# A hybrid decoder layer on one core: the first product's loads issued ahead, row loads on another queue, x scaled a chunk earlier, the keys' scale moved to the logits

## The chip, the cores and the metric

The kernel runs on one core of a Trainium2 chip. The metric is device time of one execution in microseconds; lower is better. Before the change it took 1237.17 us (median of three runs, 1237.11 to 1239.0).

## The reference

One layer of a decoder with three parallel branches: x and mem are (256, 2048), everything is float32. Only what matters here:

```python
h = rms_norm(x, norm_w);  proj = h @ w_in              # w_in: 2048 x 18464, split by columns
o_sb  = stick_breaking_attention(q, k, v) * silu(z)    # 8 heads of 128
o_ssd = gated_group_rms_norm(ssd_chunked_scan(...), z) # 32 heads, conv of 4 taps ahead
mem_n = rms_norm(mem, mem_norm_w)
kv = mem_n @ w_kv;  k, v = split(kv, 2)                # 2048 x 2048, 4 heads of 256
probs = softmax(einsum(q, k) * 256 ** -0.5);  o_mem = (probs @ v) * silu(z)
merged = g_sb * (o_sb @ w_sb) + g_ssd * (o_ssd @ w_ssd) + g_mem * (o_mem @ w_mem)
return rms_norm(x + merged @ w_out, final_norm_w)
```

## The kernel before

Every weight is read once, in chunks of 512 KB. To keep float32 precision a chunk is split: ScalarE writes its rounded high part `wh`, VectorE subtracts that from the chunk and writes the low part `wl` (`split`, L144 and L148, for scaled operands L150), and TensorE adds three products, high x high, high x low and low x high, in PSUM. A `gemm` (L238) gives 512 output columns with the tokens on the partitions: per k tile of 128 two token halves, three matmuls each (L257 to L259). A `gemm_cols` (L209) gives 256 columns transposed (L223, L227).

The order of work is written out by hand; every engine executes its instructions in that order. `gemm` and `gemm_cols` go through their chunks; each chunk loads (`load_chunk`, on SP's DMA queue), splits, multiplies and calls `pump`, which runs what has been deferred to that chunk with `defer(fn, chunks)` and one step of a queue of smaller work. A load goes into one of four buffers (`raw`, RAWB = 4) and so waits until the chunk four before has been split; `wh` and `wl` have three buffers each. Loads of all queues take turns on eight completion semaphores, so that no more than eight are in flight.

The start of the program, on which the change bears:

- The first `gemm` (memory values, columns 1024 to 1535 of `w_mem_kv`) runs over ten chunks, four of one k tile and six of two. `along0` splits the mem columns of the same k tiles (`memT`) and issues the load of the next ones. At k tile 6 it also issues two small loads, `wcols` and `drow`. From k tile 10 on each chunk issues a load of mem rows (`row_squares`), on ScalarE's DMA queue; ScalarE squares and sums them three chunks later.
- The second `gemm` (eight chunks) loads the last mem rows and four pieces of x rows in the same way (`along1`). Row tiles have two buffers of each of two kinds, so every load reuses the buffer of the row tile four loads before.
- Four `gemm_cols` give the keys `kT`. Meanwhile `scale_x` and `scale_pair` (L390) take x, transposed, through its norm, two k tiles at a time: VectorE multiplies by `rbc_x` (L392), ScalarE writes the high part of `hT`, VectorE the low part. The keys are scaled by mem's norm, `rbc_m`, as they leave PSUM (L275).
- `mem_head` (L512) reads the logits from PSUM: maximum, exponential with sum, division.
- At the end `last_cols` adds the residual and sums the squares, the last addition of `msy` on GpSimd (L857); `write_out` takes the power of it there (L863), scales in five pieces on VectorE and ScalarE and stores each.

## Time and profile before

| | |
|---|---|
| median of three runs | 1237.17 us |
| the profiled execution, its own time | 1237.6 us |
| its span, first to last instruction | 1235.9 us |
| TensorE busy | 1221.2 us (99%), 6224 matmuls |
| weight loads into TensorE busy | 1037.7 us (84%) |
| VectorE, ScalarE, GpSimd busy | 769.2 (62%), 616.6 (50%), 93.8 (8%) us |
| moved by DMA | 240.58 MB, mean 195 GB/s |
| chain that ended last, by engine | TensorE 93%, DMA 4%, VectorE 1%, ScalarE 1% |

The busy times overlap. The chain follows the execution back from its last instruction, at each step to what released it. Matmuls are pipelined: the duration of one (0.39 us for 512 columns) is longer than the step from one start to the next, and the step is what counts. "Granted clock" is the share of TensorE's full clock; 1.00 is the upper of its two levels, 2.4 GHz, and 0.5 the lower, 1.2 GHz.

### The profile page before, as it was taken

How to read it: one execution, taken by the hardware profiler on the slowest of the kernel's cores; microseconds unless marked ns; L12 is line 12 of the kernel's file. 1: busy time of each engine (PE TensorE's matmuls, PEld its weight loads, DVE VectorE, ACT ScalarE, POOL GpSimd, SP SyncE). 2: the span in 40 equal slices, each digit the busy share in tenths (PEclk: the TensorE clock that was granted, in tenths of full speed). 3: DMA queues.
4: the chain of work that ended last, by engine and by line, in shares of the span. 5: the costliest groups of instructions: out<-in, count | busy, mean ns of one | idle time of the engine just before them, and what ended most of it. 6: DMA issues, size and time to landing. Idle time of an engine off the chain costs nothing.

```text
span 1235.9 us, 16263 instructions
## 1 busy us (share of the span) xinstructions
PE 1221.2 (99%) x6224; PEld 1037.7 (84%) x6224; DVE 769.2 (62%) x995; ACT 616.6 (50%) x797; POOL 93.8 (8%) x108
## 2 busy tenths in 40 slices
PE   8999999999999999999999999999999999999996
PEld 7888888888888888888888888888888888888886
DVE  5587565455644555888878767576756554555554
ACT  6755544554444554544665655455555444444443
POOL 0000000000000000010100202023101110110101
PEclk9999999999999999999999999999999999999998
DMA  9956566654566656556566756666565666567673
GB/s 312 356 179 191 167 190 188 187 171 146 165 198 190 185 173 187 170 173 185 172 187 194 221 177 210 199 199 197 179 183 181 199 196 202 187 198 242 206 235 109
DMA packets 167869, 240.58 MB, mean 195 GB/s; under 512 B 10320, under 2 KB 93680, under 8 KB 167664
## 3 DMA queue, kind: packets, MB, share of 16 engines
q1 hardware_dynamic: 159232, 224.01, 58.7%
q10 hardware_dynamic: 8560, 15.54, 3.8%
q8 instruction: 48, 0.79, 0.3%
q14 instruction: 29, 0.24, 0.1%
HBM read 237.40 MB, written 2.13 MB: 194 GB/s over the span
## 4 chain that ended last, share of the span: by engine, by line
PE 93%; DMA 4%; DVE 1%; ACT 1%; issue 0%; SPq 0%; ACTq 0%; POOLq 0%; POOL 0%; DVEq 0%
PE acc L223 23%; PE acc L258 17%; PE acc L259 17%; PE acc L257 17%; PE acc L227 12%; PE y L741 1%; DMA raw<-in_w_mem_kv_dram 1%; DMA mraw<-in_mem_cols_dram 1%; DMA raw<-in_w_out_dram 1%; DVE wl L148 1%; DMA xraw<-in_x_cols_dram 1%; ACT wh L144 0%; PE acc L910 0%; PE off L743 0%; PE acc L912 0%; PE acc L911 0%
## 5 line engine op out<-in xcount | busy, mean ns | idle before, releaser
L148 DVE TENSOR_TENSOR wl<-raw,wh 128x1024 fp32r<-128x1024 f32 (+1 forms) x410 | 505.5, 1236 | 334.9 <-ACT wh L144 332.4
L144 ACT ACTIVATE wh<-raw 128x1024 fp32r<-128x1024 f32 (+1 forms) x410 | 431.3, 1054 | 420.4 <-PE acc L259 258.3
L223 PE MATMUL acc<-hT,wh 128*128 128x512 f32 x1152 | 363.2, 397 | 0.0
L227 PEld LDWEIGHTS acc<-hT,wl 128*128 128x128 f32 x1152 | 216.4, 188 | 51.2
L257 PE MATMUL acc<-wh,hT 128*128 128x512 f32 x576 | 227.8, 396 | 0.0
L227 PE MATMUL acc<-hT,wl 128*128 128x256 f32 x1152 | 226.6, 278 | 0.0
L259 PE MATMUL acc<-wh,hT 128*128 128x512 f32 x576 | 224.5, 390 | 0.0
L258 PE MATMUL acc<-wl,hT 128*128 128x512 f32 x576 | 224.4, 390 | 0.0
L223 PEld LDWEIGHTS acc<-hT,wh 128*128 128x128 f32 x1152 | 175.5, 189 | 0.1
L259 PEld LDWEIGHTS acc<-wh,hT 128*128 128x128 f32 x576 | 108.1, 188 | 23.0
L258 PEld LDWEIGHTS acc<-wl,hT 128*128 128x128 f32 x576 | 108.3, 188 | 21.8
L257 PEld LDWEIGHTS acc<-wh,hT 128*128 128x128 f32 x576 | 108.2, 188 | 21.6
L257 PE MATMUL acc<-wh,oD 128*128 128x512 f32 x128 | 49.8, 389 | 0.0
L258 PE MATMUL acc<-wl,oD 128*128 128x512 f32 x128 | 49.8, 389 | 0.0
L259 PE MATMUL acc<-wh,oD 128*128 128x512 f32 x128 | 49.8, 389 | 0.0
L667 DVE SCALAR_TENSOR_TENSOR cT<-cu,wcols,cT 128x255 f32<-128x255 f32 (+2 forms) x96 | 46.4, 483 | 3.4
L813 POOL TENSOR_TENSOR merged<-merged,sig 128x512 f32<-128x512 f32 x16 | 27.6, 1743 | 260.3 <-DVE sig L812 233.5
L603 POOL TENSOR_TENSOR lm<-lm,sp 128x384 f32<-128x384 f32 x8 | 11.5, 1432 | 394.5 <-DVE sp L602 392.4
L223 PE MATMUL acc<-memT,wh 128*128 128x512 f32 x128 | 40.7, 399 | 0.1
L257 PE MATMUL acc<-wh,mT 128*128 128x512 f32 x96 | 37.4, 390 | 0.0
L259 PE MATMUL acc<-wh,mT 128*128 128x512 f32 x96 | 37.4, 389 | 0.0
L258 PE MATMUL acc<-wl,mT 128*128 128x512 f32 x96 | 37.4, 389 | 0.0
(248 smaller groups left out, 1305.9 us busy)
## 6 DMA issues: line engine op xcount, KB each, us to landing
raw<-in_w_in_dram SPq DMA_DIRECT2D x288, 512.0 KB, 3.7
raw<-in_w_branch_ssd_dram SPq DMA_DIRECT2D x32, 512.0 KB, 3.9
raw<-in_w_out_dram SPq DMA_DIRECT2D x32, 512.0 KB, 4.8
raw<-in_w_mem_kv_dram SPq DMA_DIRECT2D x30, 512.0 KB, 5.7
raw<-in_w_branch_mem_dram SPq DMA_DIRECT2D x16, 512.0 KB, 4.7
raw<-in_w_branch_sb_dram SPq DMA_DIRECT2D x16, 512.0 KB, 4.0
dec<-acT ACTq DMA_DIRECT2D x16, 256.0 KB, 5.6
sig<-in_b_gate_dram ACTq DMA_DIRECT2D x12, 256.0 KB, 4.0
```

The lines of the kernel that those rows point to most:

```text
L144: nc.scalar.activation(hi, src, AF.Copy, **({} if scale is None else {"scale": scale}))
L148: nc.vector.tensor_tensor(lo, src, h32, ALU.subtract)
L223: nc.tensor.matmul(acc[:, b], wh[:, kt - k0, b * P:(b + 1) * P], lhs.both(kt), start=first, stop=False, skip_group_check=True)
L227: nc.tensor.matmul(acc[:, b, 1], wl[:, kt - k0, b * P:(b + 1) * P], lhs.at(kt)[0], start=False, stop=last, skip_group_check=True)
L257: nc.tensor.matmul(a, lh[:, tt], wh[:, j], start=first, stop=False)
L258: nc.tensor.matmul(a, lh[:, tt], wl[:, j], start=False, stop=False)
L259: nc.tensor.matmul(a, ll[:, tt], wh[:, j], start=False, stop=last)
L603: nc.gpsimd.tensor_tensor(lm, lm, sp, ALU.subtract)
L667: nc.vector.scalar_tensor_tensor(a[:, s:T], u[:, 0:T - s], convw[:, 3 - s, i:i + 1], a[:, s:T], ALU.mult, ALU.add)
L741: nc.tensor.matmul(y[:, q, xc], dec[e // 2][:, e % 2, q], xs[:, q, xc], start=True, stop=True)
L813: nc.gpsimd.tensor_tensor(merged[t][:, cs], merged[t][:, cs], sig[:, t], ALU.add)
```

## The change

It has five parts. The ten weight loads of the first `gemm` and the mem column loads are issued ahead of everything else, four of the weight loads (k tiles 4 to 11) into two tiles of their own (`own`) instead of the four shared buffers; the keys' tiles `kT` are allocated after that product. Row loads go to SP's queue, and their squares are deferred by four chunks. `scale_pair` only scales; the split of the pair follows a chunk later (`split_pair`). The keys are no longer scaled on leaving PSUM; `mem_head` multiplies the logits instead and exponentiates from that copy. In the tail the addition of `msy` moves to VectorE, the division by 2048 into the square, and the five output pieces are cut in another order.

```diff
@@ -200,8 +200,9 @@
     def silu(a, chunks=LATE):
         defer(lambda: nc.scalar.activation(a, a, AF.Silu), chunks)
 
-    def load_chunk(w, c0, width, k0, kc):
-        raw = stage.tile([P, kc, width], F32, tag="raw", name=nm("raw"), bufs=RAWB)
+    def load_chunk(w, c0, width, k0, kc, raw=None):
+        if raw is None:
+            raw = stage.tile([P, kc, width], F32, tag="raw", name=nm("raw"), bufs=RAWB)
         nc.sync.dma_start(
             raw, w[k0 * P:(k0 + kc) * P, c0:c0 + width].rearrange("(k p) n -> p k n", p=P))
         return raw
@@ -235,13 +236,13 @@
         nc.scalar.activation(dst, acc[:, :, 1], AF.Copy)
         nc.vector.tensor_tensor(dst, acc[:, :, 0], dst, ALU.add)
 
-    def gemm(lhs, nk, w, c0, evac, along=None, sizes=None):
+    def gemm(lhs, nk, w, c0, evac, along=None, sizes=None, raws=None):
 
         acc2 = psA.tile([P, 2, GW], F32, tag="acc", name=nm("acc"), bufs=2)
         acc = [acc2[:, 0], acc2[:, 1]]
         k0 = 0
         for kc in sizes or [KC] * (nk // KC):
-            raw = load_chunk(w, c0, GW, k0, kc)
+            raw = raws[k0] if raws else load_chunk(w, c0, GW, k0, kc)
             wh = stage.tile([P, kc, GW], F32R, tag="wh", name=nm("wh"))
             wl = stage.tile([P, kc, GW], F32R, tag="wl", name=nm("wl"))
             split((wh, wl, raw, None))
@@ -267,13 +268,10 @@
             fold(dst[:, b0:b0 + 2], acc)
         return evac
 
-    def to_split_cols(dst, b0, scale=None):
+    def to_split_cols(dst, b0):
         def evac(acc):
             u = tmp.tile([P, 2, T], F32, tag="cu", name=nm("u"), bufs=2)
             fold(u, acc)
-            if scale is not None:
-                nc.vector.tensor_tensor(u, u, scale.unsqueeze(1).to_broadcast([P, 2, T]),
-                                        ALU.mult)
             defer(lambda: split((*dst.at(b0, 2), u, None)), 1)
         return evac
 
@@ -307,10 +305,10 @@
         if q % 2:
             r = [ta([P, GW], "rows") for _ in range(2)]
             for t in range(2):
-                nc.scalar.dma_start(r[t], src[t * P:(t + 1) * P, cs])
+                nc.sync.dma_start(r[t], src[t * P:(t + 1) * P, cs])
             return r
         r = t4([P, 2, GW], "rows")
-        nc.scalar.dma_start(r, src[:, cs].rearrange("(t p) n -> p t n", p=P))
+        nc.sync.dma_start(r, src[:, cs].rearrange("(t p) n -> p t n", p=P))
         return [r[:, t] for t in range(2)]
 
     def squares(r, ss, q):
@@ -342,21 +340,16 @@
     ss_m = const.tile([P, 2, 4], F32, name="ss_m")
     ss_x = const.tile([P, 2, 4], F32, name="ss_x")
 
-    kT = Cols(8, "kT")
     vh = slot([P, 2, 1024], F32R, "vh")
     vl = slot([P, 2, 1024], F32R, "vl")
 
     def along0(k0):
         if k0 == 0:
             split((*memT.at(0), mem0, memw[:, 0:1]))
-            mload(1, 2)
         elif k0 < 4:
             split((*memT.at(k0), mraw[0][:, k0], memw[:, k0:k0 + 1]))
-            mload(k0 + 1, k0 + (3 if k0 == 3 else 2))
         else:
             split_cols(mraw, memT, memw, k0)
-            if k0 < 14:
-                mload(k0 + 2, k0 + 4)
         if k0 == 6:
             nc.sync.dma_start(wcols, w_cols)
             nc.sync.dma_start(drow, d_skip.partition_broadcast(P))
@@ -365,7 +358,7 @@
 
     def row_squares(src, ss, q):
         r = load_rows(src, q)
-        defer(lambda: squares(r, ss, q), 3)
+        defer(lambda: squares(r, ss, q), 4)
 
     def along1(k0):
         if k0 == 0:
@@ -391,6 +384,9 @@
         part = xraw[k // 8][:, k % 8:k % 8 + 2]
         nc.vector.tensor_tensor(part, part, rbc_x.unsqueeze(1).to_broadcast([P, 2, T]),
                                 ALU.mult)
+        defer(lambda: split_pair(k), 1)
+
+    def split_pair(k):
         split_cols(xraw, hT, normw, k)
         x_ready.append(k)
 
@@ -408,11 +404,27 @@
         defer(lambda: lanes[0].append(scale_steps(rs_mem, rbc_m, ss_m)), 1)
         defer(lambda: to_split_rows(vh, vl, 0, rs_mem)(acc), 4)
 
+
+    raws = {}
+    for k in range(4):
+        raws[k] = load_chunk(w_mem_kv, 1024, GW, k, 1)
+        mload(k + 1, k + (3 if k == 3 else 2))
+    for k in range(4, NKT, 4):
+        if k < 12:
+            own = slot([P, 4, GW], F32, "own")
+            raws[k], raws[k + 2] = own[:, 0:2], own[:, 2:4]
+        else:
+            raws[k] = raws[k + 2] = None
+        for j in (k, k + 2):
+            raws[j] = load_chunk(w_mem_kv, 1024, GW, j, 2, raws[j])
+            if j < 14:
+                mload(j + 2, j + 4)
     gemm(memT, NKT, w_mem_kv, 1024, later, along=along0,
-         sizes=[1] * 4 + [2] * 6)
+         sizes=[1] * 4 + [2] * 6, raws=raws)
+    kT = Cols(8, "kT")
     gemm(memT, NKT, w_mem_kv, 1024 + GW, to_split_rows(vh, vl, GW, rs_mem), along=along1)
     for g in range(4):
-        gemm_cols(memT, NKT, w_mem_kv, 2 * g * P, to_split_cols(kT, 2 * g, rbc_m))
+        gemm_cols(memT, NKT, w_mem_kv, 2 * g * P, to_split_cols(kT, 2 * g))
     finish()
 
 
@@ -519,14 +531,15 @@
                 nc.tensor.matmul(lg[:, t], qh, kl, start=False, stop=False)
                 nc.tensor.matmul(lg[:, t], ql, kh, start=False, stop=(d == 1))
         yield
+        pr = ta([P, 2, T], "mpr")
+        nc.vector.tensor_tensor(pr, lg, rbc_m.unsqueeze(1).to_broadcast([P, 2, T]), ALU.mult)
         mx = small([P, 2], "mx")
-        nc.vector.tensor_reduce(mx, lg, AX.X, ALU.max)
+        nc.vector.tensor_reduce(mx, pr, AX.X, ALU.max)
         nmx = small([P, 2], "nmx")
         nc.vector.tensor_scalar(nmx, mx, -1.0 / 16.0, None, ALU.mult)
-        pr = ta([P, 2, T], "mpr")
         sums = small([P, 2], "sums")
         for t in range(2):
-            nc.scalar.activation(pr[:, t], lg[:, t], AF.Exp, bias=nmx[:, t:t + 1],
+            nc.scalar.activation(pr[:, t], pr[:, t], AF.Exp, bias=nmx[:, t:t + 1],
                                  scale=1.0 / 16.0, accum_out=sums[:, t:t + 1])
         rec = small([P, 2], "rec")
         nc.vector.reciprocal(rec, sums)
@@ -853,18 +866,17 @@
                                     ALU.add)
             junk = tq([P, T], "junk")
             q = ssy[:, t, 3 + c // T:4 + c // T]
-            nc.scalar.activation(junk, yc, AF.Square, accum_out=q)
-            nc.gpsimd.tensor_scalar(msy[:, t:t + 1], q, 1.0 / D, msy[:, t:t + 1], ALU.mult,
-                                    ALU.add)
+            nc.scalar.activation(junk, yc, AF.Square, scale=D ** -0.5, accum_out=q)
+            nc.vector.tensor_tensor(msy[:, t:t + 1], q, msy[:, t:t + 1], ALU.add)
             nc.vector.tensor_tensor(yc, yc, fw[:, 3 * GW + c:3 * GW + c + T], ALU.mult)
 
     def write_out(t):
         rs = small([P, 1], "frs")
         nc.gpsimd.tensor_tensor(rs, msy[:, t:t + 1], mhalf[:, 0:1], ALU.pow)
-        for c0, c1, eng, dma in ((0, 512, nc.vector, nc.sync), (512, 896, nc.scalar, nc.scalar),
-                                 (896, 1408, nc.vector, nc.sync),
-                                 (1408, 1664, nc.scalar, nc.scalar),
-                                 (1664, 2048, nc.vector, nc.sync)):
+        for c0, c1, eng, dma in ((0, 256, nc.vector, nc.sync), (256, 640, nc.scalar, nc.scalar),
+                                 (640, 1152, nc.vector, nc.sync),
+                                 (1152, 1536, nc.scalar, nc.scalar),
+                                 (1536, 2048, nc.vector, nc.sync)):
             o = yo[t][:, c0:c1]
             if eng is nc.vector:
                 eng.tensor_scalar(o, o, rs, None, ALU.mult)
```

The tables below show the order of instructions before and after at the places that the prediction speaks of. On SP's DMA queue, from the end of the first product's loads on (`mraw` mem columns, `raw_246` to `raw_321` weights of the first product, `raw_348` and later those of the second), before:

```order
L361 DMA wcols<-in_w_cols_dram 128x192
L362 DMA drow<-in_d_skip_dram 128x32
L205 DMA raw_246<-in_w_mem_kv_dram 128x2x512
L297 DMA mraw_125<-in_mem_cols_dram 128x512
L205 DMA raw_269<-in_w_mem_kv_dram 128x2x512
L297 DMA mraw_125<-in_mem_cols_dram 128x512
L205 DMA raw_294<-in_w_mem_kv_dram 128x2x512
L297 DMA mraw_125<-in_mem_cols_dram 128x512
L205 DMA raw_321<-in_w_mem_kv_dram 128x2x512
L205 DMA raw_348<-in_w_mem_kv_dram 128x2x512
L205 DMA raw_372<-in_w_mem_kv_dram 128x2x512
```

The same place now (`raw_160` is the first product's last weight load, `raw_344`, `raw_368` and `raw_390` are the second product's first three; `rows` the mem and x rows):

```order
L206 DMA raw_160<-in_w_mem_kv_dram 128x2x512
L354 DMA wcols<-in_w_cols_dram 128x192
L355 DMA drow<-in_d_skip_dram 128x32
L311 DMA rows_281<-in_mem_dram 128x2x512
L308 DMA rows_303<-in_mem_dram 128x512
L308 DMA rows_304<-in_mem_dram 128x512
L311 DMA rows_327<-in_mem_dram 128x2x512
L206 DMA raw_344<-in_w_mem_kv_dram 128x2x512
L308 DMA rows_350<-in_mem_dram 128x512
L308 DMA rows_351<-in_mem_dram 128x512
L206 DMA raw_368<-in_w_mem_kv_dram 128x2x512
L311 DMA rows_374<-in_x_dram 128x2x512
```

The two small loads stand behind all of the first product's loads, and the rows, which were on ScalarE's queue, stand between the weights. `raw_390` follows the last row shown.

On VectorE, while x is scaled (`xraw` is x, `wl` the low part of a weight chunk, `hT` the split of x, `u` the keys on leaving PSUM), before:

```order
L392 TENSOR_TENSOR xraw_126<-xraw_126,rbc_x 128x512
L150 SCALAR_TENSOR_TENSOR hT_120<-xraw_126,wcols,hT_120 128x256 x2
L148 TENSOR_TENSOR wl_674<-raw_671,wh_673 128x1024
L392 TENSOR_TENSOR xraw_126<-xraw_126,rbc_x 128x512
L150 SCALAR_TENSOR_TENSOR hT_120<-xraw_126,wcols,hT_120 128x256 x2
L236 TENSOR_TENSOR u_698<-acc_541,u_698 128x512
L275 TENSOR_TENSOR u_698<-u_698,rbc_m 128x512
L148 TENSOR_TENSOR wl_705<-raw_702,wh_704 128x1024
L148 TENSOR_TENSOR kT_130<-u_698,kT_130 128x2x256
```

And now:

```order
L385 TENSOR_TENSOR xraw_126<-xraw_126,rbc_x 128x512
L148 TENSOR_TENSOR wl_668<-raw_665,wh_667 128x1024
L385 TENSOR_TENSOR xraw_126<-xraw_126,rbc_x 128x512
L237 TENSOR_TENSOR u_688<-acc_539,u_688 128x512
L150 SCALAR_TENSOR_TENSOR hT_120<-xraw_126,wcols,hT_120 128x256 x2
L148 TENSOR_TENSOR wl_698<-raw_695,wh_697 128x1024
L150 SCALAR_TENSOR_TENSOR hT_120<-xraw_126,wcols,hT_120 128x256 x2
L148 TENSOR_TENSOR kT_341<-u_688,kT_341 128x2x256
```

Between scaling a pair and splitting it there is now a chunk's low part, and the multiplication by `rbc_m` is gone.

## Rows read from the trace of the kernel before

**Rows 1.** Stretches: length, busy by engine, granted clock, DMA share, GB/s.
```profile
0.00:8.00 8.00, 5.83 (x25) 5.02 (x26) 2.65 (x5) 4.44 (x8) 1.85 (x12) 1.00 0.71 236
8.00:14.50 6.50, 4.92 (x20) 3.41 (x19) 3.53 (x7) 2.99 (x6) 0.00 (x0) 1.00 0.96 280
14.50:18.00 3.50, 3.50 (x9) 2.72 (x9) 2.11 (x4) 2.23 (x4) 0.00 (x0) 0.51 1.02 379
18.00:24.00 6.00, 6.00 (x28) 4.96 (x27) 5.48 (x9) 5.12 (x10) 0.00 (x0) 1.00 1.02 368
24.00:40.00 16.00, 16.00 (x72) 13.25 (x71) 7.39 (x10) 12.23 (x28) 0.00 (x0) 1.00 1.02 356
40.00:48.00 8.00, 7.55 (x33) 5.93 (x32) 3.60 (x6) 6.04 (x13) 0.71 (x1) 1.00 1.05 400
```

**Rows 2.** TensorE's timeline, first two groups: start, us, line, operation, [idle before <-releaser].
```profile
5.75 0.50 PE L257 MATMUL acc<-wh,memT 128*128 128x512 f32 x1 [1.14 <-ACT memT L144]
13.00 0.49 PE L257 MATMUL acc<-wh,memT 128*128 128x512 f32 x1 [1.22 <-ACT memT L144]
14.64 0.63 PE L257 MATMUL acc<-wh,memT 128*128 128x512 f32 x1
18.22 0.39 PE L257 MATMUL acc<-wh,memT 128*128 128x512 f32 x1
45.45 0.39 PE L257 MATMUL acc<-wh,memT 128*128 128x512 f32 x1
46.29 0.50 PE L258 MATMUL acc<-wl,memT 128*128 128x512 f32 x1 [0.45 <-DVE wl L148]
54.64 0.60 PE L332 MATMUL rbc<-dg,ones 128*128 128x256 f32 x2
```

**Rows 3.** ScalarE's timeline before the late chunk.
```profile
42.69 0.63 ACT L318 ACTIVATE rows<-rows 128x512 f32<-128x512 f32 x1 [1.85 <-DMA xraw<-in_x_cols_dram]
43.93 1.04 ACT L144 ACTIVATE wh<-raw 128x1024 fp32r<-128x1024 f32 x1
```

**Rows 4.** VectorE's timeline while x is scaled.
```profile
90.28 0.88 DVE L150 SCALAR_TENSOR_TENSOR hT<-xraw,wcols,hT 128x256 fp32r<-128x256 f32 x2 [0.58 <-ACT hT L144]
91.62 1.23 DVE L148 TENSOR_TENSOR wl<-raw,wh 128x1024 fp32r<-128x1024 f32 x1 [0.47 <-ACT wh L144]
93.48 0.69 DVE L275 TENSOR_TENSOR u<-u,rbc_m 128x512 f32<-128x512 f32 x1
```

**Rows 5.** TensorE's timeline while x is scaled.
```profile
91.75 0.62 PE L223 MATMUL acc<-memT,wh 128*128 128x512 f32 x2
92.90 0.39 PE L227 MATMUL acc<-memT,wl 128*128 128x256 f32 x1 [0.53 <-DVE wl L148]
98.38 0.73 PE L223 MATMUL acc<-memT,wh 128*128 128x512 f32 x2
99.64 0.50 PE L227 MATMUL acc<-memT,wl 128*128 128x256 f32 x2 [0.52 <-DVE wl L148]
```

**Rows 6.** VectorE's and GpSimd's timelines in the tail.
```profile
1214.86 0.15 DVE L847 TENSOR_SCALAR msy<-fs 128x1 f32<-128x1 f32 x1
1228.61 0.42 POOL L857 TENSOR_SCALAR msy<-ssy,msy 128x1 f32<-128x1 f32 x1 [5.15 <-ACT junk L856]
1229.71 1.21 DVE L870 TENSOR_SCALAR yo<-yo,frs 128x512 f32<-128x512 f32 x3 [0.81 <-POOL frs L863]
```

**Rows 7.** SP's timeline: the second small load, the first group's last weight load.
```profile
8.89 1.10 SPq L362 DMA_DIRECT2D drow<-in_d_skip_dram  x1
16.64 0.38 SPq L205 DMA_DIRECT2D raw<-in_w_mem_kv_dram  x1
```

**Rows 8.** DMA issues at 16.64 and at 51.98: count, KB each, us to landing.
```profile
raw<-in_w_mem_kv_dram SPq DMA_DIRECT2D x1, 512.0 KB, 6.5
raw<-in_w_mem_kv_dram SPq DMA_DIRECT2D x1, 512.0 KB, 3.7
```

**Rows 9.** The stretch of the memory heads (columns of group 1).
```profile
250.00:330.00 80.00, 80.00 (x493) 71.31 (x492) 45.64 (x60) 37.38 (x56) 0.00 (x0) 1.00 0.56 167
```

## The prediction

> **What bounds the kernel now.** I read the busy time by stretch first, then TensorE's timeline wherever a matmul started late, then the engines named as having ended those waits, then the DMA landings, and last the chain after the final matmul. In [rows 1] TensorE is busy for all 16 us of the stretch from 24 to 40, and so it goes through nearly the whole kernel: only time in which it waits, or runs slowly, can be given back. Three places have such time.
>
> The first is the start. In [rows 2] the first matmul begins at 5.75 us, and the second group's row of matmuls ends at 54.64. The two groups have 192 matmuls of 512 columns; from 18.22 to 45.45 there are 120 of them, 0.227 us each. Without a wait they would end at 5.75 + 192 x 0.227 = 49.3, so 5.3 us are lost. Some 2 us go at k tile 4: idle for 1.22 us before the matmul at 13.00, and again for its low part, which splits later. The clock follows: 0.51 from 14.5 to 18.0 in [rows 1], half speed, where a matmul shows 0.63 us; 3.5 us at that level cost 3.5 x 0.49 = 1.7 us. One late chunk of the second group, at 46.29, costs 0.6 [rows 2].
>
> What stands behind these waits is the DMA queue: its share in [rows 1] is 0.96 to 1.05 from 8 us to 48 us. The bytes moved are, by these rows, 1.89 MB at 8 us, 3.71 at 14.5, 5.03 at 18, 7.24 at 24, 12.94 at 40, 16.1 at 48. The late chunk at 46.29 is an in-order effect on top: ScalarE stood still until 42.69 for a row tile before it could start the split at 43.93 [rows 3].
>
> The second place is the scaling of x. VectorE waits 0.58 us for ScalarE's high part between scaling and subtracting, and then 0.47 for the split of the next weights, which stood behind that high part on ScalarE [rows 4]. TensorE's two low-part matmuls at 92.90 and 99.64 come late [rows 5]. The third place is the tail after the last matmul [rows 6].
>
> **The change, part by part.**
>
> *Early loads (term A).* The first ten weight loads and nine loads of mem columns now stand first on SP's queue, then the two small loads, then three mem row loads, and only then the second group's weights, each with a row load beside it. No byte is saved. The DMA engines were full anyway, so what counts is the order. I add up what stands ahead of a load and look for that amount in the delivery of [rows 1]. A load lands later than its bytes alone say: the first group's last weight load was issued at 16.64 and took 6.5 us [rows 7, 8], so it landed at 23.1; 6.41 MB were issued up to it, 6.91 MB were delivered then, a lag of 0.5 MB.
>
> For the second group's first weight load: 0.14 (head) + 4.19 (weights) + 1.97 (mem columns) + 0.12 (small) + 1.57 (three row loads) + 0.52 (itself) = 8.51 MB, with the lag 9.01: 24 + (9.01 - 7.24) / 0.356 = 29.0 us. For its sixth (k tile 10): 8.51 + 5 x 0.524 (weights) + 5 x 0.524 (rows) = 13.75, with the lag 14.25: 40 + (14.25 - 12.94) / 0.400 = 43.3 us. The split needs 1.06 on ScalarE [rows 3] and 1.23 on VectorE [rows 4], so the low part is there at 45.6; the chunk starts a matmul earlier, at 45.4, and three chunks of 12 x 0.227 = 2.72 remain: end at 53.5 instead of 54.64. **A = -1.1 us.** Squares deferred by a chunk more (3 to 4) belong to it: ScalarE no longer meets a row tile that has not landed, because that row now stands ahead of the weights on the same queue.
>
> The bounds of A are far apart. Best, TensorE never waits in the two groups: -5.3. Worst, the second rival below: +5.4. I take -1.1 since it rests on the delivery that the trace has.
>
> In these rows weights and rows share the DMA engines whoever issued them: the share stays near 1 from 24 to 40, when both queues are in use [rows 1]. The Trainium skill, "DMA: Bandwidth & Descriptors", section "Issuing engines are not separate DMA queues", says that transfers started by different engines run on the same 16 DMA engines, and that a second issuing engine only saves issue time. By that rule the move of the row loads is worth nothing by itself, and A would be 0; the first rival takes this up.
> The same page of the Trainium skill, "DMA: Bandwidth & Descriptors", gives under "Specifications" about 358 GB/s as the HBM limit of a core; [rows 1] have 400 over 8 us, so the measurement decides. At 358 the sixth load would land 0.4 us later and A would be -0.7.
>
> *x a chunk ahead (term B).* From [rows 5]: the step 91.75 to 92.90 is 1.15 where two matmuls of 512 columns take 0.46, so 0.69 is lost; 98.38 to 99.64 is 1.26, so 0.80. Together 1.5, and 0.26 more just before 98.38 that I do not count. The new order puts a weight split between scaling and subtracting, so that each of the eight pairs drops 0.58 + 0.47 us of VectorE's waits [rows 4], and the scale at the logits removes four multiplications of 0.69 us from this same stretch: 8 x 1.05 + 4 x 0.69 = 11.2 us of VectorE's time in some 40 us, many times the 1.5 lost. **B = -1.5 us.** Bounds: -1.8 (all that is lost there) and 0 (another wait ends last). hT gets its last pair a chunk (2.8 us) later; its reader, the fourth chunk of the next product, comes three chunks after the memory products end, so no one waits.
>
> *Scale at the logits (term C).* Four multiplications of 0.69 move to the memory heads. VectorE is busy 45.64 of 80 us there and TensorE 80.00 of 80 [rows 9]. Hidden: **C = 0**; uncovered, it would be 4 x 0.69 = 2.8 us.
>
> *Tail (term D).* GpSimd's 0.42 us addition [rows 6] becomes a VectorE addition on one column, for which the 0.15 us operation of [rows 6] is the nearest row. The power operation (pow) waits for it; with two handovers of some 0.05 us, 0.4 - 0.15 + 0.1 = 0.35 to 0.4 is saved. The first piece to be scaled is 256 columns instead of 512: three pieces take 1.21 us, 0.4 each [rows 6]; I estimate 0.25 for half the size between 0.15 and 0.4, another 0.15. The output's bytes and piece sizes are the same five, only in another order. **D = -0.5 us**, between 0 (the last piece bounds) and -0.6.
>
> **Sum.** -1.1 - 1.5 + 0 - 0.5 = -3.1 us. The profiled execution took 1237.6 us (span 1235.9), so 1234.5 by its own time; the median of the three runs is 1237.17, 0.4 below it: **1234.1 us**. About 0.2% (2.5 us) is what a measurement of this kernel can tell from no change, so the forecast lies just beyond that, on the faster side.
>
> **The rivals.**
> 1. *Order alone buys nothing early.* The share near 1 speaks for it; also that the second group's first load now has 1.57 MB of rows ahead of it, which the kernel before loaded beside it. Then A = 0 and the time is 1237.2 - 2.0 = 1235.2: no change. The rule of the Trainium skill cited above comes to this time. Against it: the late chunk's 0.6 us came from ScalarE's order, which does change. Chance 0.28.
> 2. *SP's queue is held by its own row loads: slower.* A row load of x must wait until the tile's earlier row is squared, and the next weights stand behind it on SP. Let the second group's first weights land at t = 29.0. Split (1.06) and two squares (0.63 each, [rows 3]) end at t + 2.3. Only then do the x rows go, and the weights of k tile 4 behind them. A load on an almost empty queue takes 3.7 us [rows 8], of which some 1.3 is transfer, so k tile 4 lands at about t + 2.3 + 3.7 + 1.3 = t + 7.3 and can be multiplied at t + 9.4; TensorE wants it at t + 2.1 + 2 x 2.72 = t + 7.5. That is 1.9 us, and the same comes again four k tiles on. The group then ends 27.5 after t, at 56.5: +1.9. If each pause is followed by a stretch at half clock as in [rows 1] (1.7 each), +5.4; with B and D that gives 1237.2 + 5.4 - 2.0 = 1240.6. It decides if the DMA queue holds less than 2.3 us of work, 0.8 MB, at t. At t one row load and one weight load are ahead, 1.05 MB less the lag of 0.5: on the edge. Against it: a wait this close moves by the lag alone. Chance 0.10.
> 3. *The slow stretch goes.* 280 GB/s from 8 to 14.5 is the lowest full stretch of [rows 1], and the small load issued at 8.89 took 1.10 us to issue instead of 0.38 [rows 7]. If the small loads caused it, 6.5 x (0.368 - 0.280) = 0.57 MB come 1.6 us sooner and k tile 4 in time, and the half clock goes with it. A then is between -1.1 - 1.6 = -2.7 and -5.3; halfway, at -4.0, the time is 1237.2 - 6.0 = 1231.2. Against it: DMA shares stayed at 0.96, and nothing shows those loads to be the cause. Chance 0.17.
>
> **How the numbers follow.** My forecast has 0.45, mostly faster, a fifth of it within 0.2%. Faster: 0.36 + 0.17 + a little of rival 1 = 0.56. Same: 0.09 + 0.25 + a little of rival 2 = 0.35. Slower: 0.09. The range goes from 1230.5 (rival 3) to 1238.0, which takes in rival 1 with C partly uncovered and the milder half of rival 2; about 2 in 10 stays out.
>
> **What would show it.** A: the sixth weight load of the second group lands near 43.3 and the group's last matmul ends near 53.5; a pause of 2 us at k tile 4 of the second group, with SP waiting for ScalarE's squares, means rival 2. B: no idle time at the low-part matmuls where 92.90 and 99.64 stood, and no 0.58 us waits on VectorE. D: the power starts 0.35 to 0.4 us sooner after the last matmul. C is wrong if TensorE idles between 250 and 330 us. I am wrong altogether if the first 55 us move by more than 3 us either way.

## The result, and the profile after

The changed kernel took 1239.56 us (median of 20 runs, 1238.22 to 1241.78) beside 1237.20 for the kernel before on the same chips (20 runs, 1235.72 to 1239.03): ratio 1.0019, interval 1.0012 to 1.0026, that is 2.4 us slower (by the interval 1.5 to 3.2). The prediction was 1234.1 us, faster. The profiled execution took 1240.05 us by its own time, its span is 1238.3 (before 1235.9).

Line numbers of the profile after are those of the changed kernel: weight loads L206, row loads L308 and L311, squares L316, the first two products' matmuls L258 to L260. First the busy time by stretch, with the columns of [rows 1]:

```profile
8.00:14.50 6.50, 6.26 (x23) 4.59 (x22) 4.11 (x7) 4.35 (x8) 0.00 (x0) 1.00 1.01 364
14.50:18.00 3.50, 3.50 (x16) 2.86 (x16) 3.50 (x7) 3.37 (x6) 0.00 (x0) 1.00 1.06 408
24.00:28.00 4.00, 4.00 (x20) 3.30 (x19) 1.40 (x3) 0.14 (x1) 0.00 (x0) 1.00 0.96 368
28.00:32.00 4.00, 3.88 (x17) 2.91 (x16) 1.26 (x2) 3.41 (x7) 0.00 (x0) 1.00 0.10 35
32.00:40.00 8.00, 5.48 (x23) 3.96 (x22) 2.42 (x2) 3.58 (x10) 0.00 (x0) 1.00 0.78 257
40.00:48.00 8.00, 6.18 (x25) 4.33 (x24) 2.78 (x4) 4.42 (x10) 0.71 (x1) 0.97 0.90 299
48.00:55.00 7.00, 7.00 (x26) 5.59 (x26) 4.19 (x6) 6.32 (x13) 0.00 (x0) 0.79 1.05 397
```

Two things differ from [rows 1]. The slow stretch has gone: 364 GB/s from 8 to 14.5 us where there were 280, and full clock from 14.5 to 18. (This one pair of profiles does not show that the early loads gave the clock back; see e5 and e8 below.) And from 28 to 32 us the DMA engines stand idle, share 0.10, in the middle of a product that waits for weights; after it TensorE is busy 5.48 of 8 and 6.18 of 8 us. SyncE's DMA queue from 20 to 50 us says why (first two rows of its waits: total, times, longest):

```profile
SPq L311 <- ACT rows L316: 12.9, 2, 7.7
SPq L308 <- ACT rows L316: 2.6, 4, 1.3
```

Two loads of x rows, L311, stood there for 12.9 us, one of them for 7.7, until ScalarE had squared the rows that lay in their tile. The queue itself in the same place:

```profile
19.80 0.38 SPq L206 DMA_DIRECT2D raw<-in_w_mem_kv_dram  x1
21.04 0.82 SPq L308 DMA_DIRECT2D rows<-in_mem_dram  x2
21.96 0.38 SPq L206 DMA_DIRECT2D raw<-in_w_mem_kv_dram  x1
30.69 0.38 SPq L311 DMA_DIRECT2D rows<-in_x_dram  x1
31.16 0.42 SPq L206 DMA_DIRECT2D raw<-in_w_mem_kv_dram  x1
```

Nothing is issued between 22.3 and 30.69. The weights of k tile 4 leave only at 31.16, directly behind the row load. ScalarE tells what the row load waited for:

```profile
28.38 1.06 ACT L144 ACTIVATE wh<-raw 128x1024 fp32r<-128x1024 f32 x1 [4.23 <-DMA raw<-in_w_mem_kv_dram]
29.34 0.61 ACT L316 ACTIVATE rows<-rows 128x512 f32<-128x512 f32 x1
29.95 0.61 ACT L316 ACTIVATE rows<-rows 128x512 f32<-128x512 f32 x1
36.95 1.06 ACT L144 ACTIVATE wh<-raw 128x1024 fp32r<-128x1024 f32 x1 [3.80 <-DMA raw<-in_w_mem_kv_dram]
48.45 1.06 ACT L144 ACTIVATE wh<-raw 128x1024 fp32r<-128x1024 f32 x1 [1.20 <-DMA raw<-in_w_mem_kv_dram]
```

The squares stand behind the split of the second product's first chunk, and that chunk's weights landed only at 28.3, when ScalarE had been idle for 4.2 us. (The last line is the split of its sixth chunk.) It is a ring: squares behind weights on ScalarE, row load behind squares, next weights behind the row load on SP. TensorE pays at k tile 4 and again four k tiles on:

```profile
38.06 0.50 PE L258 MATMUL acc<-wh,memT 128*128 128x512 f32 x1 [1.76 <-ACT wh L144]
39.33 0.50 PE L259 MATMUL acc<-wl,memT 128*128 128x512 f32 x1 [0.76 <-DVE wl L148]
46.08 0.50 PE L258 MATMUL acc<-wh,memT 128*128 128x512 f32 x1 [1.06 <-ACT wh L144]
47.34 0.64 PE L259 MATMUL acc<-wl,memT 128*128 128x512 f32 x1 [0.76 <-DVE wl L148]
59.74 0.60 PE L330 MATMUL rbc<-dg,ones 128*128 128x256 f32 x2
```

Against a step of 0.227 the first four cost 1.92 + 1.04 + 1.22 + 1.03 = 5.2 us, and eight steps at half speed after the second pause 1.6 more (clock 0.79 from 48 to 55). The second product ends at 59.74 instead of 54.64 [rows 2].

In the memory heads there are two pauses that the kernel before does not have, at 275.91 us and in the same way at 316.52:

```profile
275.04 0.63 PE L224 MATMUL acc<-hT,wh 128*128 128x512 f32 x2
275.91 0.50 PE L228 MATMUL acc<-hT,wl 128*128 128x256 f32 x2 [0.24 <-DVE wl L148]
```

The step of 0.87 should be 0.45. VectorE's timeline has the cause, the new multiplication in a run of small operations that ends just before three weight splits in a row:

```profile
270.91 0.68 DVE L535 TENSOR_TENSOR mpr<-mlg,rbc_m 128x512 f32<-128x512 f32 x1
271.62 0.69 DVE L537 TENSOR_REDUCE mx<-mpr 128x2 f32<-128x512 f32 x1
273.88 0.62 DVE L547 TENSOR_SCALAR mpr<-mpr,rec 128x256 f32<-128x256 f32 x2
274.63 3.50 DVE L148 TENSOR_TENSOR wl<-raw,wh 128x1024 fp32r<-128x1024 f32 x3
```

The account of the two profiled executions: the first two products +5.1; from there to the end of the x stage (TensorE's `dtr` matmul, 144.81 before, 147.94 after) -2.0; the heads +1.05; a wait of TensorE before the last output columns that the profile of before shows and that of after does not, -1.2 (it comes and goes in the profiles below, 0.2 to 0.9 us of idle time, in kernels that don't touch it); after the last matmul 8.2 instead of 8.7, -0.5. The sum is +2.45, the difference of the spans.

### The profile page after: what moved, and what is told of

It reads as the page before. It is cut to its first block, busy times and chain, and to the rows that moved or that the text cites. A ratio compares the mean times of both kernels' runs of the same rounds, so it can differ in the third digit from the quotient of the medians.

```text
span 1238.3 us, 16254 instructions
## 1 busy us (share of the span) xinstructions
PE 1223.4 (99%) x6224; PEld 1039.1 (84%) x6224; DVE 770.0 (62%) x999; ACT 617.4 (50%) x797; POOL 92.4 (7%) x104
## 4 chain that ended last, share of the span: by engine, by line
PE 93%; DMA 3%; ACT 1%; DVE 1%; issue 1%; SPq 0%; POOLq 0%; POOL 0%; ACTq 0%; DVEq 0%
PE acc L224 24%; PE acc L259 17%; PE acc L260 17%; PE acc L258 17%; PE acc L228 12%; DMA raw<-in_w_mem_kv_dram 2%; PE y L754 1%; DMA raw<-in_w_out_dram 1%; ACT wh L144 1%; DMA own<-in_w_mem_kv_dram 1%; DVE wl L148 0%; PE off L756 0%; DMA head<-in_mem_cols_dram 0%; PE dtp L445 0%; PE dot L784 0%
## 5 line engine op out<-in xcount | busy, mean ns | idle before, releaser
L258 PE MATMUL acc<-wh,hT 128*128 128x512 f32 x576 | 227.8, 395 | 0.0
L260 PE MATMUL acc<-wh,hT 128*128 128x512 f32 x576 | 224.5, 390 | 0.0
L260 PEld LDWEIGHTS acc<-wh,hT 128*128 128x128 f32 x576 | 108.1, 188 | 22.9
L258 PEld LDWEIGHTS acc<-wh,hT 128*128 128x128 f32 x576 | 108.2, 188 | 21.7
L258 PE MATMUL acc<-wh,oD 128*128 128x512 f32 x128 | 49.8, 389 | 0.0
L260 PE MATMUL acc<-wh,oD 128*128 128x512 f32 x128 | 49.8, 389 | 0.0
L258 PE MATMUL acc<-wh,mT 128*128 128x512 f32 x96 | 37.4, 390 | 0.0
L260 PE MATMUL acc<-wh,mT 128*128 128x512 f32 x96 | 37.4, 389 | 0.0
```

Of the source, the lines that this page charges most:

```text
L258: nc.tensor.matmul(a, lh[:, tt], wh[:, j], start=first, stop=False)
L260: nc.tensor.matmul(a, ll[:, tt], wh[:, j], start=False, stop=last)
```

## The experiments

All times are medians. The kernels were timed in three sessions, each with the kernel before beside them, which took 1237.12, 1237.19 and 1237.31 us; it took 1237.20 beside the change. A ratio of 0.9990 is 1.2 us.

| kernel | us | ratio to before, interval |
|---|---|---|
| the change | 1239.56 | 1.0019, 1.0012 to 1.0026 |
| e1 rows on ScalarE's queue | 1234.02 | 0.9973, 0.9963 to 0.9983 |
| e2 squares three chunks later | 1234.40 | 0.9978, 0.9969 to 0.9986 |
| e12 x rows in tiles of their own | 1233.83 | 0.9971, 0.9960 to 0.9983 |
| e3 before + rows on SP, squares four | 1242.38 | 1.0042, 1.0030 to 1.0055 |
| e4 before + early loads | 1235.40 | 0.9990, 0.9981 to 0.9999 |
| e5 before + x ahead | 1235.13 | 0.9987, 0.9978 to 0.9996 |
| e6 before + scale at the logits | 1236.78 | 1.0000, 0.9991 to 1.0009 |
| e7 before + small loads late | 1235.71 | 0.9990, 0.9980 to 0.9999 |
| e8 = e1 + keys scaled as before | 1232.40 | 0.9966, 0.9955 to 0.9978 |
| e9 = e8 + small loads early | 1233.31 | 0.9967, 0.9954 to 0.9979 |
| e10 = e8 + six single chunks | 1231.60 | 0.9954, 0.9941 to 0.9966 |
| e11 = e8 + squares three | 1232.34 | 0.9966, 0.9952 to 0.9979 |

**e1.** The change, with the row loads on the other queue:

```diff
-                nc.sync.dma_start(r[t], src[t * P:(t + 1) * P, cs])
+                nc.scalar.dma_start(r[t], src[t * P:(t + 1) * P, cs])
-        nc.sync.dma_start(r, src[:, cs].rearrange("(t p) n -> p t n", p=P))
+        nc.scalar.dma_start(r, src[:, cs].rearrange("(t p) n -> p t n", p=P))
```

> The change with its row loads back on ScalarE's queue (squares still four chunks later). Theory (SP's queue is held: the x row loads wait on SP for squares that ScalarE makes after the split of the second product's first chunk, and the next weights wait behind them): the weights no longer wait, the DMA engines no longer fall idle near 28 us, the 5.1 us lost by the start of the third group go; 1239.5 - 4 to 5 = 1234.5 to 1235.5, the fast stretch at 8 to 14.5 us stays (360 GB/s). Rival R1 (loads issued early are themselves at fault: rows and weights of the second product stand too far behind): still 1238.5 to 1240. Rival R2 (what counts is only the bytes ahead of a load): between, about 1237.

1234.02 us, 5.5 below the change. The stretch that stood idle is full, and the second product ends at 52.42:

```profile
28.00:32.00 4.00, 4.00 (x19) 3.32 (x18) 1.28 (x2) 3.48 (x8) 0.00 (x0) 1.00 1.05 408
```

**e2.** The change, with one number other:

```diff
-        defer(lambda: squares(r, ss, q), 4)
+        defer(lambda: squares(r, ss, q), 3)
```

> The change with one number other: squares deferred by three chunks instead of four, row loads still on SP's queue. Theory (held queue): the squares that the first x row load waits for now stand on ScalarE ahead of the split of the second product's first chunk and not behind it, so the row load goes as soon as the mem rows have landed, and the weights of k tile 4 go with it: no pause at k tile 4 of the second product, 1234.5 to 1236.5. If the row loads on SP cost by their place among the weights whatever the squares do (R2), 1238.5 to 1240 as the change. If the early loads are at fault (R1), also 1238.5 to 1240.

1234.40 us. The row loads are still on SP, but the first squares now run before the first chunk's split and the queue moves on. On SP's queue, the row load and the weights of k tile 4, 5.4 us sooner than in the change:

```profile
25.25 0.38 SPq L311 DMA_DIRECT2D rows<-in_x_dram  x1
25.72 0.42 SPq L206 DMA_DIRECT2D raw<-in_w_mem_kv_dram  x1
```

**e12.** The change, queue and squares as they are, but the x rows in tiles that nobody has to free (and each piece of them in one load):

```diff
+        if src is x:
+            r = slot([P, 2, GW], F32, "xrows")
+            nc.sync.dma_start(r, src[:, cs].rearrange("(t p) n -> p t n", p=P))
+            return [r[:, t] for t in range(2)]
```

> The change, row loads still on SP's queue and squares still four chunks later, but the four x row loads go into tiles of their own instead of the mem rows' tiles, so that none of them waits for squares. Theory (the queue is held by the row loads' wait for their tiles): no pause at k tile 4 of the second product, DMA busy from 28 to 32 us, and the time of the two kernels that remove the hold in other ways: 1234 to 1235. If the place of the rows among the weights or the later squares cost the 5 us, it stays at 1238.5 to 1240.

1233.83 us, and no wait of SP for squares of `rows` between 20 and 50 us. From 28 to 32 us:

```profile
28.00:32.00 4.00, 3.51 (x15) 2.56 (x15) 1.26 (x2) 3.42 (x7) 0.00 (x0) 1.00 1.05 408
```

Three edits that have in common only the end of that wait give back 5.2 to 5.7 us, each 0.1 to 0.5 us more than was expected of it. The place of the rows among the weights (kept in e2 and e12) and the later squares (kept in e1 and e12) are not the cause by themselves: it takes the row loads on SP, in tiles that must be freed, and squares late enough to stand behind the weights.

**e3 and e4** take the start apart on the kernel before. e3 has the two edits of the rows alone (queue SP, squares four chunks later), e4 the early loads and own tiles alone.

> The kernel before with this part of the change alone: row loads on SP's queue, squares four chunks later. Theory (held queue): the row loads wait for squares here too, and the weights behind them; SP stands still for some microseconds in the second product, but the DMA queue is still behind here (it was full until 48 us), so part of the wait is covered: 1238 to 1241, slower than before by 1 to 4. Rival R1 (early loads at fault): 1237.2, no change. A rival that the queue's move helps: 1236.

> The kernel before with the other part of the start alone: the first product's loads issued ahead and in tiles of their own; row loads stay on ScalarE's queue, squares three chunks later. Theory: the slow stretch from 8 to 14.5 us goes (280 to about 360 GB/s) with the late matmul at 13.0 and the half clock from 14.5 to 18, and no queue is held: 1237.2 - 2 to 4 = 1233 to 1235.2. Rival R1 (early loads at fault for the loss in the second product): 1238 to 1241.

e3: 1242.38 us, 5.2 slower than before; more than expected, for the work still queued in the kernel before was no cover. The same wait and the same idle stretch:

```profile
SPq L313 <- ACT rows L318: 12.1, 2, 6.9
```

```profile
28.00:32.00 4.00, 4.00 (x18) 3.09 (x17) 2.10 (x5) 3.43 (x7) 0.00 (x0) 1.00 0.21 71
```

e4: 1235.40, ratio 0.9990, so the early loads alone gain 1.2 us (0.1 to 2.4), a little less than I expected from their faster delivery (386 GB/s from 8 to 14.5 us, full clock after it): one chunk of its second product still came late, 1.7 us at 43.67. The hold needs only the queue and the late squares, in the tiles as they were; the early loads are not at fault.

**e5 and e6** take the x stage apart, again on the kernel before. e5 defers the split of a pair of x by a chunk, e6 moves the keys' scale to the logits:

```diff
-        split_cols(xraw, hT, normw, k)
-        x_ready.append(k)
+        defer(lambda: split_pair(k), 1)
```

```diff
-        gemm_cols(memT, NKT, w_mem_kv, 2 * g * P, to_split_cols(kT, 2 * g, rbc_m))
+        gemm_cols(memT, NKT, w_mem_kv, 2 * g * P, to_split_cols(kT, 2 * g))
...
+        nc.vector.tensor_tensor(pr, lg, rbc_m.unsqueeze(1).to_broadcast([P, 2, T]), ALU.mult)
```

> The kernel before with only the split of a pair of x deferred by a chunk behind its scaling; the keys are still scaled on leaving PSUM. If the order of VectorE's work is what made the two low-part matmuls late (term B), both pauses (0.70 and 0.81 us, and 0.26) go: 1237.1 - 1.5 to 1.8 = 1235.4. Rival: VectorE's time in that stretch is short, and the four multiplications that stay keep a pause: 1236 to 1237.

> The kernel before with only the keys' scale moved to the logits. Theory from the trace of the changed kernel: the multiplication lengthens VectorE's chain before a weight split, TensorE waits twice for a low part in the memory heads (0.42 us and 0.12 behind it, each): +0.8 to +1.1; the pauses in the x stage stay: 1238.0. The prediction's C = 0 gives 1237.1. Rival: four multiplications fewer in the x stage end the pauses there: 1236.2 to 1236.5.

e5: ratio 0.9987, -1.6 us (-2.7 to -0.5); between 85 and 105 us its TensorE waits for nothing any more, where the kernel before waited twice [rows 5]. e6: ratio 1.0000. Its trace holds a gain and a loss. In the x stage the steps of 1.15 and 1.26 are gone but for one of 0.79 (-1.5 us), and both pauses of the heads are there (+1.0; the last two lines show the first of them); the rest is less than the interval of 1.1 us either way can tell:

```profile
97.37 0.63 PE L223 MATMUL acc<-memT,wh 128*128 128x512 f32 x2
98.16 0.51 PE L227 MATMUL acc<-memT,wl 128*128 128x256 f32 x2 [0.15 <-DVE wl L148]
270.42 0.63 PE L223 MATMUL acc<-hT,wh 128*128 128x512 f32 x2
271.29 0.50 PE L227 MATMUL acc<-hT,wl 128*128 128x256 f32 x2 [0.24 <-DVE wl L148]
```

Both my theory of e6 and its rival were half right. In the change the split a chunk later had already ended the pauses of the x stage, so the scale at the logits had nothing left to gain there, and only its loss remained.

**e8** is e1 with the keys scaled on leaving PSUM as before the change.

> The change with its row loads on ScalarE's queue (1234.0) and the keys scaled on leaving PSUM again. If the scale at the logits costs the two pauses seen in the memory heads, they go: 1234.0 - 0.8 to 1.1 = 1233.0 to 1233.2, and the x stage stays without pauses. If the multiplication in the x stage brings the pauses back there (+1.5) the time is 1234.5; if C is nothing, 1234.0.

1232.40 us, 1.6 below e1 (the intervals overlap) and 0.6 lower than was expected; no wait of TensorE for VectorE from 85 to 105 us nor from 250 to 330, so the heads' 1.05 is gone in the trace and the pauses of the x stage don't come back.

**e7 and e9** ask whether the two small loads cause the slow stretch: e7 issues them later in the kernel before, e9 puts them early into e8.

```diff
-        if k0 == 6:
-            nc.sync.dma_start(wcols, w_cols)
-            nc.sync.dma_start(drow, d_skip.partition_broadcast(P))
...
+        if k0 == 10:
+            nc.sync.dma_start(wcols, w_cols)
+            nc.sync.dma_start(drow, d_skip.partition_broadcast(P))
```

> The kernel before with the two small loads (wcols, drow) issued in the second product at k tile 10 instead of the first at k tile 6; nothing else. If these loads cause the slow stretch (rival 3 of the prediction), the profile shows 340 to 390 GB/s from 8 to 14.5 us and the time is that of the early loads alone, 1235.4. If it is how late the weights and mem columns are issued (each a chunk ahead of its use, behind buffers), the stretch stays at 280 to 320 GB/s and the time at 1237.1.

> The fastest kernel so far (the change with rows on ScalarE's queue and the keys scaled on leaving PSUM, 1232.4) with the two small loads back at their place behind k tile 6's weights. If they slow the DMA in the first product (rival 3), 8 to 14.5 us shows 280 to 300 GB/s instead of 338 to 364 and the time rises by 1 to 2: 1233.5 to 1234.5. If not, 1232.4 and 330 GB/s or more.

The stretch from 8 to 14.5 us in e7, in e8 and in e9, in this order:

```profile
8.00:14.50 6.50, 4.75 (x20) 3.19 (x19) 3.90 (x7) 3.68 (x7) 0.00 (x0) 1.00 0.98 320
```

```profile
8.00:14.50 6.50, 4.81 (x21) 3.42 (x19) 3.64 (x7) 3.83 (x8) 0.00 (x0) 1.00 0.98 338
```

```profile
8.00:14.50 6.50, 6.14 (x23) 4.41 (x22) 4.17 (x8) 4.47 (x9) 0.00 (x0) 1.00 0.90 306
```

Over all profiles, the five with the small loads at their old place have 280, 282, 287, 306 and 319 GB/s there, the nine others 320 to 386. Both edits moved the rate the way the small loads would, but neither result is clear. e7's 320 is the top of the range that was to speak against the small loads, though its time is nearer to the reading that blames them; e9's 306 GB/s and 1233.31 us lie between its two readings. With one profile each, and e3 (loads at the old place) at 319 beside e7's 320, it is likely and not shown that those loads slow the stretch. What rival 3 hung on it did not follow. In e7 TensorE still waits for k tile 4, and half clock comes after it:

```profile
13.13 0.50 PE L257 MATMUL acc<-wh,memT 128*128 128x512 f32 x1 [1.40 <-ACT memT L144]
```

```profile
14.50:18.00 3.50, 3.50 (x9) 2.79 (x10) 3.13 (x5) 3.22 (x6) 0.00 (x0) 0.54 1.05 400
```

Nor does the clock go with the early loads: e5, whose start is that of the kernel before, has full clock in the same stretch, and e8, with the early loads, has half. First e5, then e8:

```profile
14.50:18.00 3.50, 3.50 (x15) 2.74 (x16) 2.58 (x5) 1.35 (x3) 0.00 (x0) 1.00 0.94 344
14.50:18.00 3.50, 3.50 (x9) 2.61 (x10) 3.50 (x6) 3.18 (x6) 0.00 (x0) 0.52 1.05 408
```

In time, e7 gains 1.2 us (0.1 to 2.5), but in its profile the second product begins at 32.00 us where that of before has 31.85, so the first product shows no gain there. e9 and e8 cannot be told apart. What the small loads cost is left open.

**e10** splits the first product's k tiles 4 and 5 into chunks of their own, on e8:

```diff
...
     gemm(memT, NKT, w_mem_kv, 1024, later, along=along0,
-         sizes=[1] * 4 + [2] * 6, raws=raws)
+         sizes=[1] * 6 + [2] * 5, raws=raws)
```

The loads issued ahead, left out here, are cut to match.

> The same fastest kernel with the first product cut into six chunks of one k tile and five of two (before: four and six), so that k tile 4 needs 256 KB of weights instead of 512 and a split of 0.63 us instead of 1.06. If the last pause of the start (0.9 to 1.5 us at k tile 4 and the half clock behind it in some runs) hangs on that chunk's size: 1230.5 to 1231.5. If the delivery as a whole is short there, the pause moves to k tile 6 and the time stays at 1232.4.

1231.60 us, the fastest here: ratio 0.9954, 5.7 us below before and 8.0 below the change. TensorE runs without a wait from 5.72 to 14.51 us; a shorter pause has moved to k tile 6, so both readings were partly right:

```profile
14.51 0.49 PE L258 MATMUL acc<-wh,memT 128*128 128x512 f32 x1
15.37 0.50 PE L259 MATMUL acc<-wl,memT 128*128 128x512 f32 x1 [0.37 <-DVE wl L148]
```

Its interval overlaps that of e8.

**e11** is e8 with the squares three chunks later instead of four.

> The same fastest kernel with the squares three chunks later, as before the change. With early loads alone and squares after three chunks one chunk of the second product was late, as ScalarE stood still for a row tile (0.65 + 1.03 us at 43.67): that comes back, 1232.4 + 1.7 = 1234.1. If the deferral does nothing with the rows on ScalarE's queue, 1232.4.

1232.34: my expectation failed. The late chunk that e4 showed at 43.67 does not come back, and with the rows on ScalarE's queue the deferral by four is worth nothing that can be measured. What made e4's chunk late was not tried further.

## Why the prediction was wrong

**A, the early loads, -1.1 predicted, +5.1 in the trace.** This is the step that failed. The prediction booked "Squares deferred by a chunk more (3 to 4) belong to it" as a free part of the gain and left the ring that it closes to the second rival, with a chance of 0.10. Its mechanism, place and pauses came as written there: the row load went 2.4 us after the first weights landed (28.27, 30.69; 2.3 worked out), k tile 4's first matmul waited 1.8 us (1.9 worked out), again four k tiles on, and the time worked out was 1240.6 beside 1239.56. That the time came so near is in part luck: the rival's sum has two stretches at half clock, where one came, and not the 1.0 us that TensorE waited for the low part in each pause. The forecast's own sum let a load land as soon as the bytes ahead of it had been moved; by it the sixth weights of the second product were due near 43.3, and ScalarE had them at 48.45.

What was wrong was the weighing. At t, the prediction said, "one row load and one weight load are ahead, 1.05 MB less the lag of 0.5: on the edge". That leaves 0.55 MB, and the rival's condition was "less than 2.3 us of work, 0.8 MB": by the prediction's own numbers it held, and the chance of 0.10 does not follow from them. The lag was too small besides. The profile after has 9.5 MB delivered at 28 us (each stretch's GB/s times its length) and 35 GB/s from then on; all that had been issued before the hold is 8.51 + 2 x 0.52 = 9.56 MB. So the first weights landed when nearly everything behind them was in as well: the lag was 1.0 MB, not 0.5, and there was no cover. The trace tells how. Each load has 16 completions there. Of the first weights' 16, fifteen had come by 26.52 and the last came at 28.27; of the second weights', 29.11 and 30.77. Meanwhile the share of the 16 DMA engines is 0.06, that of one engine:

```profile
28.80:30.40 1.60, 1.60 (x9) 1.18 (x7) 0.93 (x1) 1.60 (x4) 0.00 (x0) 1.00 0.06 24
```

So the lag was here one part of a load that came 1.7 us behind the others, and no fixed number of MB; why it trailed is not shown. The prediction had read its lag from a single load, whose last completion came only 0.26 us behind the others (22.84, 23.10); other loads of the kernel before trail by up to 1.75 us (29.18, 30.93). With either lag the rival should have been the forecast.

**Rival 3 came in part.** The rate rose as it said, to 364 GB/s, and the first weights landed at 28.3 instead of 29.0. Its cause is not shown, and e7, without the small loads there, still had the late k tile 4 and the half clock. I had set the two rivals against each other, though nothing excludes both. e3 shows the hold with 319 GB/s, so faster delivery did not create it.

**Rival 1** fell in e1: the queue alone is worth 5.5 us. The Trainium skill, "DMA: Bandwidth & Descriptors", section "Issuing engines are not separate DMA queues", has that a second issuing engine saves only issue time. Its shared engines agree with e1, where the DMA share is 1.05 with loads on both queues. What decided here was SP's program order, where a load that waits for its tile keeps every later load from being issued, 12.9 us in all.

**B, x a chunk ahead, -1.5 predicted.** Right: -2.0 in the trace (the bound was -1.8) and -1.6 measured alone in e5, with the waits gone as said. But it was reckoned as the work of the two edits together; in their traces e5 alone ends all of these pauses and e6 alone three quarters (-1.5 of -2.0).

**C, the scale at the logits, 0 predicted.** Wrong by 1.05: [rows 9] showed VectorE busy 45.64 of 80 us and I took that for cover. The share hid a run of VectorE's operations that ends just in time for a weight split; 0.69 us more and the split was late. "C is wrong if TensorE idles between 250 and 330 us" did happen: 79.52 of 80 us busy.

**D, the tail, -0.5.** Right in this pair of profiles: GpSimd's power starts 1.56 us after the last matmul's start (1230.12) instead of 1.96, 0.4 sooner as worked out, and the end comes 0.5 us sooner. GpSimd's timeline of the profile after:

```profile
1231.68 0.68 POOL L875 TENSOR_TENSOR frs<-msy,mhalf 128x1 f32<-128x1 f32 x1 [9.14 <-DVE msy L870]
```

The tail was not run alone, since 0.5 us is below what these runs tell.

Without the hold the sum came out, partly by luck: e1, the whole change but for the queue, took 1234.02 beside 1234.1 predicted. In its profile the first two products end 2.2 us sooner than before (A said 1.1) and the x stage gains 2.0 (B said 1.5), and C's loss of 1.05 takes most of that back.

## What to carry to other kernels

Before loads are moved to a queue, write down for each what it waits for, and what stands behind it there: a load that reuses a buffer makes every later load wait for that buffer's reader, and if the reader stands behind one of those loads' data on its own engine the two form a ring that empties the DMA engines. When a rival's condition comes out "on the edge", check on which side its own numbers fall, and work out its bounds from more than one row, before it is given a small chance. A busy share of 57% was no cover here for work that goes into a chain which ends just ahead of a deadline.

## What was unexpected of the hardware

A load landed only when nearly all the bytes issued after it had been moved too, 8.51 MB in order and 9.5 MB delivered, because the last of its 16 completions came 1.75 us after the other fifteen. The rate over whole stretches was 397 to 410 GB/s in many of these profiles.

A granted clock of 1.00 in a stretch does not always mean that it was measured. In the profile after, matmuls of 512 columns step by 0.43 us in both of these places, twice the usual 0.227; the row of the first stretch reads 1.00, that of the second 0.51. TensorE's timeline, and the stretches:

```profile
7.02 0.63 PE L258 MATMUL acc<-wh,memT 128*128 128x512 f32 x1
7.44 0.63 PE L259 MATMUL acc<-wl,memT 128*128 128x512 f32 x1
```

```profile
7.00:10.00 3.00, 3.00 (x8) 2.31 (x7) 2.38 (x6) 2.06 (x4) 0.00 (x0) 1.00 0.93 286
49.00:51.00 2.00, 2.00 (x6) 1.56 (x5) 1.46 (x3) 1.77 (x6) 0.00 (x0) 0.51 1.05 405
```

The trace's own records of the granted clock settle it. The first one, 1.00, begins at 9.99 us, just where the steps fall from 0.42 to 0.24; ahead of it there is none, and the row counts such time as 1.00. The record of 0.5 runs from 47.54 to 50.95. In the kernel before the first record begins at 4.28 us, and its matmuls ran at full speed from 6.81 on (a step of 0.23); in e2, e5, e6, e9 and e11 it begins between 8.99 and 10.33, with the slow steps ahead of it. What decides how long the slow start lasts was not tried.
